# A diagonal state-space layer in blocks of four steps, with a turned scan over 128 blocks

## The chip, the cores and the metric

The kernel runs on one core of one Trainium2 chip. The metric is the device time of one execution in microseconds; the profile is one execution as the hardware profiler recorded it. PE is TensorE's matmul, PEld its weight load, DVE is VectorE, ACT ScalarE, POOL GpSimd, SP SyncE.

## The reference

A batch of one, 512 tokens, width 1024, in float32. Two layers of block 1 (neighbourhood attention, grouped attention, spatial gating, merged by gates) are followed by one layer of block 2. Block 2 projects the tokens to three branches of width 512: forgetting attention, a chunked state-space scan, and the diagonal state-space layer that is changed here. The gated sum of the branches is projected and normed; a convolutional feed-forward part ends the program. The diagonal layer has 32 groups of 16 channels with 64 complex states each:

```python
mag = jnp.exp(lam_re * step)
abar_re = mag * jnp.cos(lam_im * step)
abar_im = mag * jnp.sin(lam_im * step)
...
bu_re = jnp.einsum('blgh,gnh->lbgn', ug, bb_re)
bu_im = jnp.einsum('blgh,gnh->lbgn', ug, bb_im)
...
_, _, h_re, h_im = lax.associative_scan(
    _complex_linear_combine, (a_seq_re, a_seq_im, bu_re, bu_im), axis=0)
y = (jnp.einsum('lbgn,ghn->blgh', h_re, c_re.astype(f32))
     - jnp.einsum('lbgn,ghn->blgh', h_im, c_im.astype(f32)))
y = y.reshape(bsz, l, S5_WIDTH) + d_skip.astype(f32) * u.astype(f32)
gy = jax.nn.gelu(y)
out = gy * jax.nn.sigmoid(gy @ w_glu.astype(f32) + b_glu.astype(f32))
```

So each complex state follows h[t] = a h[t-1] + B u[t], over 512 steps, and y = Re(C h) + d u.

## The kernel before

Nearly all products are taken in two exact parts: `load_w` (L67) loads weights, ScalarE rounds the high part (L76), VectorE or GpSimd (by `lo_gp`) takes the low part (L78), and `mm3` (L99 to L101) issues three fp32r matmuls of 128 weights by 512 tokens per product. Sums go to PSUM banks by tag: three of "mm", two of "s", two of "t", one of "v". Tiles of 128 x 512 come from one pool ("b2", 36 buffers), tables and rows from another ("ld", 7). All DMAs are issued on SyncE.

Independent work is written as Python generators and interleaved by hand: `fill` (L165) advances a queue of projection jobs, and `step` advances the state-space branch. Within what the dependencies and the pools allow, a planner at compile time orders the instructions of each engine; every engine then takes its own queue in order.

`s5_params` (L1125) prepares the branch. It is a generator, advanced by the merges of block 1, one piece per 128 output columns. It computes magnitudes and phases, tables of cos and sin over 128 steps for the 16 tiles of 128 states (GpSimd, L1214 to L1222, to DRAM), the input matrices in two parts ("lbd") and the output matrices ("cc5").

`s5` (L1286) is advanced by block 2: 0.9 pieces per step of `fox`, 0.4 per step of `ssd`, 0.8 per step of the merges (RF, RS, RM). Each of 16 tiles of states takes: two input matmuls over 512 tokens (L1326), whose three stacked parts of the inputs are put together by small DMAs (L1315); a turn by the phase tables (L1331 to L1337, VectorE and GpSimd), which makes the recurrence real; eight scans of 128 steps with the magnitude as factor (L1355), with a carry between the four pieces of the sequence (L1347 to L1351); a turn back (L1362 to L1368); and output matmuls with 32 columns of fp32 weights (L1376). After every fourth tile comes the gelu. `prep` projects the inputs of four tiles and splits them.

`block2` (L1435) runs `fox`, `ssd`, the merges of branches 0 and 1, what is left of `s5`, then `glu` and the merge of branch 2. In a merge, L726 takes the gates and L741 empties a product's "mm" bank on VectorE. At the end of block 1 and later, `ln_tok` norms each token tile with a power on GpSimd (L247).

Of the kernel before, what the change touches and what calls it, by code (L numbers as in the profile page):

```python
# [19 lines left out]
P = 128  # L20
# [5 lines left out]
class Net:  # L26
    def __init__(self, ctx, tc, a, out, dump=None, upto=99):
# [11 lines left out]
        # weights' low parts: which of them GpSimd takes from VectorE, in turn  # L39
# [27 lines left out]
    def load_w(self, src):  # L67
        """weights in two exact parts"""
# [25 lines left out]
    def mm3(self, ps, ws, xs, first=True, last=True):  # L94
        """ps += sum over k of w^T x, with w and x in two exact parts each"""
# [7 lines left out]
    def fm(self, src, w=None):  # L103
        """features x tokens tile [128, 512] of x @ w for 128 columns of w"""
# [6 lines left out]
    def fm2(self, srcs):  # L111
        """two such tiles, by halves of the tokens"""
# [8 lines left out]
    def tm(self, srcs, use):  # L121
        """tokens x 256 columns tiles of x @ w; use(t, psum)"""
# [42 lines left out]
    def fill(self, n=1, drain=False):  # L165
        """advances the first of the queued generators"""
# [132 lines left out]
    def weights_T(self, e, n):  # L299
        """[128 queries, n keys] -> [128 keys, n / 128, 128 queries]"""  # L300
# [8 lines left out]
    def heads_q(self, src, scale=1.0):  # L309
        """fp32 [128,512] holding two heads -> per head 64 rows of high and 64 rows of low parts"""  # L310
# [9 lines left out]
    def heads_k(self, src):  # L320
        """the same for the keys: per head the high parts in both halves; the low parts of both heads"""
# [10 lines left out]
    def z_gate(self, bias_name, bi, out):  # L332
        """use of a projection tile: z * (1 + tanh(z / 2)) = 2 silu(z) goes into out, z = psum + b"""
# [10 lines left out]
    def gqa(self, l, zs):  # L344
        """zs: the gates, times which the outputs go into zs"""
# [3 lines left out]
        # values of two token tiles: [high 0, low 0, low 1, high 1] for the groups 0 and 1  # L349
# [36 lines left out]
        # rotation tables times the norms' gains: [128, 2 (cos|sin), 4, 64] for q and k  # L386
# [8 lines left out]
        def norm_rope(u, tc_, ts_, split):  # L395
            """[128, 8, 64] -> two tiles [128, 4, 2, 64] with each head twice"""
# [32 lines left out]
        def q_T(qo):  # L429
            qs = []  # L430
            for i in range(2):
# [3 lines left out]
                # rows 0-63 the high parts, rows 64-127 the low parts  # L435
# [15 lines left out]
        # heads in pairs of one group: their weights go through the values together  # L451
# [16 lines left out]
        def turn(i):  # L468
            """two key tiles of a pair's weights -> [128 keys, 2 tiles, (2 heads, 128 queries)], two parts"""
# [18 lines left out]
        def gate(t, i):  # L488
            """the sums' two parts, the bias and the gates of heads i, i + 1 and i + 4, i + 5"""
# [76 lines left out]
    def sgu(self, l, vn, uz, ys):  # L566
        """a generator"""
# [22 lines left out]
    def na(self, l, vd):  # L590
# [45 lines left out]
        def bias(i):  # L636
            """the relative positions' bias with the mask for step i"""
# [78 lines left out]
    def merge_gen(self, out, r, ys, wbr, gates, bname, b0, first=False, last=False, step=None):  # L716
        """acc += (1 + tanh(gate / 2)) * (y @ w) for one branch; the last gives the sum in two parts"""
# [150 lines left out]
    def bcast_row(self, ps, r, last=True):  # L868
        """ps[m, t] = row r of the cumulative sums, for every m"""
# [4 lines left out]
    def fox(self, xb, zz, step):  # L874
# [41 lines left out]
        js += [zj(i) for i in range(4)]  # L916
        self.queue.append(self.jobs(js))
# [7 lines left out]
        def weights(hp, t, s):  # L925
# [13 lines left out]
            # scores less the keys' sums; the query's sum is added to the maximum and to the exponent's bias  # L939
# [46 lines left out]
    def conv(self, ps, col, k, bias):  # L986
        """causal depthwise convolution over the tokens of a features x tokens tile"""
# [7 lines left out]
    def ssd(self, xb, zz, step):  # L995
# [3 lines left out]
        # ends of the chunks, on every partition  # L999
# [500 lines left out]
NB2 = 36  # L1500
# [177 lines left out]
```

## Time and profile before

| | before |
|---|---|
| median of 3 runs | 2070.54 us |
| lowest to highest | 2069.55 to 2071.32 us |
| span of the profiled execution | 2068.7 us |
| median of the runs less that span | 1.8 us |
| PE, DVE, ACT, POOL busy | 1996.5, 1407.4, 859.7, 515.1 us |
| mean granted TensorE clock | 0.989 |

The profile has no time of its own for the profiled execution beside its span, so its time is taken as the span and 1.8 us. Busy time of an engine is the union of its records; a matmul's records overlap, so 0.389 us long ones can follow each other every 0.225 us. Stretches are in us from the span's start. Block 2 begins at about 1120, and the merge of branch 2 ends at about 1650.

### The profile page before, as it was taken

How to read it: one execution, taken by the hardware profiler on the slowest of the kernel's cores; microseconds unless marked ns; L12 is line 12 of the kernel's file. 1: busy time of each engine (PE TensorE's matmuls, PEld its weight loads, DVE VectorE, ACT ScalarE, POOL GpSimd, SP SyncE). 2: the span in 40 equal slices, each digit the busy share in tenths (PEclk: the TensorE clock that was granted, in tenths of full speed). 3: DMA queues.
4: the chain of work that ended last, by engine and by line, in shares of the span. 5: the costliest groups of instructions: out<-in, count | busy, mean ns of one | idle time of the engine just before them, and what ended most of it. 6: DMA issues, size and time to landing. Idle time of an engine off the chain costs nothing. (4 is left out here: it accounts for less than half of the span.)

```text
span 2068.7 us, 29389 instructions
## 1 busy us (share of the span) xinstructions
PE 1996.5 (97%) x10402; PEld 1641.8 (79%) x10402; DVE 1407.4 (68%) x2857; ACT 859.7 (42%) x1742; POOL 515.1 (25%) x542
## 2 busy tenths in 40 slices
PE   7999999999999999999999999998979999999998
PEld 7898877788899888777888776766657888888888
DVE  7776646764667674567447688879997476645655
ACT  3455446433334553654233555532223334423431
POOL 3343211101324436123001334537660000000000
PEclk9999999999999999999999999999989999999999
DMA  6432233334343322333444222212313423333332
GB/s 211 150 98 72 74 97 106 106 94 126 117 153 90 99 74 82 110 112 124 137 126 148 83 70 69 73 34 93 91 62 111 132 85 106 96 97 97 101 86 69
DMA packets 127699, 209.88 MB, mean 101 GB/s; under 512 B 15936, under 2 KB 33344, under 8 KB 127552
## 3 DMA queue, kind: packets, MB, share of 16 engines
q1 hardware_dynamic: 127552, 208.01, 32.3%
q8 instruction: 82, 1.34, 0.3%
q14 instruction: 65, 0.53, 0.1%
HBM read 190.65 MB, written 14.16 MB: 99 GB/s over the span
## 5 line engine op out<-in xcount | busy, mean ns | idle before, releaser
L99 PE MATMUL psmm<-xh,wh 128*128 128x512 f32 (+1 forms) x1504 | 605.0, 403 | 32.2 <-DVE tmp L741 19.3
L76 ACT CAST wh<-wr 128x512 fp32r<-128x512 f32 x605 | 362.1, 618 | 605.5 <-PE psmm L100 296.1
L78 DVE TENSOR_TENSOR wl<-wr,wh 128x512 fp32r<-128x512 f32 x525 | 369.5, 714 | 334.4 <-ACT wh L76 330.5
L100 PE MATMUL psmm<-xl,wh 128*128 128x512 f32 (+1 forms) x1504 | 590.0, 392 | 0.3 <-DVE xl L262 0.3
L101 PE MATMUL psmm<-xh,wl 128*128 128x512 f32 (+1 forms) x1504 | 589.4, 392 | 0.0
L99 PEld LDWEIGHTS psmm<-xh,wh 128*128 128x128 f32 x1504 | 285.2, 190 | 97.8 <-DVE tmp L741 20.6
L101 PEld LDWEIGHTS psmm<-xh,wl 128*128 128x128 f32 x1504 | 284.7, 189 | 61.5 <-DVE wl L78 1.4
L100 PEld LDWEIGHTS psmm<-xl,wh 128*128 128x128 f32 x1504 | 285.7, 190 | 53.8 <-DVE xl L262 0.7
L247 POOL TENSOR_TENSOR sm<-sm,mhalf 128x1 f32<-128x1 f32 x20 | 18.9, 946 | 711.6 <-DVE sm L245 711.6
L100 PE MATMUL psmm<-wl,xh 128*128 128x256 f32 (+1 forms) x512 | 147.2, 288 | 2.8 <-DVE wl L78 2.5
L99 PE MATMUL psmm<-wh,xh 128*128 128x256 f32 (+1 forms) x512 | 148.1, 290 | 0.9 <-ACT xh L261 0.8
L101 PE MATMUL psmm<-wh,xl 128*128 128x256 f32 (+1 forms) x512 | 147.4, 288 | 0.3 <-DVE xl L262 0.2
L78 POOL TENSOR_TENSOR wl<-wr,wh 128x512 fp32r<-128x512 f32 x80 | 113.7, 1433 | 113.6 <-ACT wh L76 104.8
L465 POOL TENSOR_SCALAR b<-b,sm 128x512 f32<-128x512 f32 x64 | 100.4, 1570 | 163.9 <-DVE sm L296 147.7
L99 PE MATMUL psmm<-b,wh 128*128 128x512 f32 x304 | 120.2, 395 | 0.1
L100 PE MATMUL psmm<-b,wh 128*128 128x512 f32 x304 | 118.7, 390 | 0.0
L101 PE MATMUL psmm<-b,wl 128*128 128x512 f32 x304 | 118.5, 390 | 0.0
L100 PEld LDWEIGHTS psmm<-wl,xh 128*128 128x128 f32 x512 | 99.5, 194 | 4.8 <-DVE wl L78 3.6
L99 PEld LDWEIGHTS psmm<-wh,xh 128*128 128x128 f32 x512 | 99.4, 195 | 2.7 <-ACT xh L261 1.5
L101 PEld LDWEIGHTS psmm<-wh,xl 128*128 128x128 f32 x512 | 99.4, 194 | 0.8 <-DVE xl L262 0.8
L294 ACT ACTIVATE b<-pss,sm 128x512 f32<-128x512 f32 x64 | 44.1, 688 | 82.3 <-DVE sm L291 81.8
L647 POOL TENSOR_TENSOR b<-ld,namask 128x256 f32<-128x256 f32 x48 | 39.6, 850 | 154.2 <-PE pss L659 30.7
(375 smaller groups left out, 3495.3 us busy)
## 6 DMA issues: line engine op xcount, KB each, us to landing
wr<-in_w1fm SPq DMA_DIRECT2D x192, 256.0 KB
wr<-in_w2fm SPq DMA_DIRECT2D x92, 256.0 KB
wr<-in_wup SPq DMA_DIRECT2D x88, 256.0 KB
wr<-in_wbr SPq DMA_DIRECT2D x72, 256.0 KB
wr<-in_w1tm SPq DMA_DIRECT2D x56, 256.0 KB
wr<-in_wout SPq DMA_DIRECT2D x48, 256.0 KB
wr<-in_wdown SPq DMA_DIRECT2D x43, 256.0 KB
ld<-in_rows SPq DMA_DIRECT2D x32, 256.0 KB
```

What stands on the lines that cost most here:

```text
L76: nc.scalar.copy(hi[:, c], raw)
L78: eng.tensor_tensor(lo[:, c], raw, hi[:, c].bitcast(F32), op=ALU.subtract)
L99: mm(ps, wh, xh, start=(first and k == 0), stop=False)
L100: mm(ps, wh, xl, start=False, stop=False)
L101: mm(ps, wl, xh, start=False, stop=(last and k == n - 1))
L247: nc.gpsimd.tensor_tensor(rs, ve, self.mhalf[:, :1], op=ALU.pow)
L294: nc.scalar.activation(e[:, :n], src, AF.Exp, bias=nm, scale=scale, accum_out=sm)
L465: nc.gpsimd.tensor_scalar(e, e, r, None, op0=ALU.mult)
L647: nc.gpsimd.tensor_tensor(bms[i][:, s], bts[hp][s][:, :, x0:x0 + 32], self.namask[:, (0, 1, 1, 2)[j], None].to_broadcast([P, 8, 32]), op=A ...
```

## The change

The sequence is cut in 128 blocks of BT = 4 steps. A tile of inputs is regrouped so that its 128 partitions are 4 steps by 32 channels and its columns are the blocks. Input matrices ("lbd") hold B, aB, a^2 B, a^3 B, so one matmul of 128 rows gives what a block adds to a state; the scan runs over 128 blocks with the magnitude to the fourth and phase tables of the fourth power; output matrices ("cbd") give the four steps' outputs from the state at the block's start, and a triangular matrix ("dbd", the skip weight on its diagonal) gives the part inside the block. Four tiles of states go through one instruction of 512 columns, with a factor of zero at each tile's first block in place of carries. These matmuls are plain fp32, no longer in parts. The input projections become jobs of the queue in `fox`, and inputs and outputs are regrouped by writing them to DRAM ("usd", "ysd") and reading them back in another order. Preparation gains the matrices' powers, on VectorE and GpSimd, and small matmuls. The pool "b2" has 43 buffers, the pieces per step are 0, 0.5 and 1.5, and the compiler's scratch for DMAs of GpSimd is set to 1024 bytes.

```diff
@@ fox: the jobs of the queue
         js += [zj(i) for i in range(4)]
+        def uj(F):
+            return self.fm_job(fm[18 + F], lambda ps: self.s5_in(F, ps))
+        self.ub = {}
+        js += [uj(F) for F in range(4)]
...
+    def s5_in(self, F, pu):
+        nc = self.nc
+        u = self.b2()
+        nc.scalar.copy(u.rearrange("p (j b) -> p b j", j=BT), pu.rearrange("p (b j) -> p b j", j=BT))
+        nc.sync.dma_start(self.usd[F], u)
+        ub = self.b2(shape=(P, 4, P))
+        src = self.usd[F].rearrange("(i r) (j b) -> j r i b", r=32, j=BT)
+        for j in range(BT):
+            nc.sync.dma_start(ub[32 * j:32 * j + 32], src[j])
+        self.ub[F] = ub
@@ s5_params, after the tables
+        def cmul(eng, o, x, y, neg=False):
+            u1, u2 = (self.tmp(shape=(P, 16, 16)) for _ in range(2))
+            eng.tensor_tensor(u1, x[0], y[0], op=ALU.mult)
...
+        for j in range(BT - 1, -1, -1):
+            for h in range(2):
+                blk = self.b2(shape=(P, 2, 2, 2, 64))
+                for k in range(2):
...
+                    g.tensor_tensor(blk[:, :, k], src[:, :, None].to_broadcast([P, 2, 2, 64]), par.to_broadcast([P, 2, 2, 64]), op=ALU.mult)
+                for f in range(2):
+                    nc.sync.dma_start(self.lbd[2 * h + f, :, 32 * j:32 * j + 32], blk[:, f].rearrange("p k g n -> p (k g n)"))
+            if j:
+                nxt = self.b2(shape=(P, 2, 16, 16))
+                cmul(v, (nxt[:, 0], nxt[:, 1]), wide[2:], (cur[:, 0], cur[:, 1]))
+                cur = nxt
+            yield
...
+        cmul(g, (bd[:, 0], bd[:, 1]), tall[:2], (bn[:, 0], bn[:, 1]))
...
+        for k in range(BT):
+            nxt = self.b2(shape=(P, 2, 16, 16))
+            cmul(g, (nxt[:, 0], nxt[:, 1]), tall[2:], (ck[-1][:, 0], ck[-1][:, 1]), neg=True)
+            ck.append(nxt)
             yield
...
         for F in range(4):
...
+                spread(e0[:, 0, k], bd[:, k], F)
+                spread(e0[:, 1, k], ck[0][:, k], F)
+                for j in range(BT):
+                    spread(ce[k][:, :, j], ck[j + 1][:, k], F)
             yield
+            pl = self.psum("mm", (P, P))
+            for i in range(4):
+                for k in range(2):
+                    nc.tensor.matmul(pl[32 * i:32 * i + 32, 0:32], e0[:, 0, k, i].rearrange("p g c -> p (g c)"),
+                                     e0[:, 1, k, i].rearrange("p g c -> p (g c)"), start=(k == 0), stop=(k == 1))
...
@@ s5
+        for F in range(4):
+            while F not in self.ub:
+                self.fill(1)
+            ub = self.ub.pop(F)
+            mt = self.b2(shape=B4)
+            gp.tensor_copy(mt, self.magb[:, 4 * F:4 * F + 4, None].to_broadcast(list(B4)))
+            gp.memset(mt[:, :, 0:1], 0.0)
+            px = [self.psum(tags[0]) for _ in range(2)]
             for k in range(2):
+                for i in range(4):
+                    nc.tensor.matmul(px[k][:, i * P:i * P + P], w[i // 2][:, i % 2, k * P:k * P + P], ub[:, i], start=True, stop=True)
...
+            for x in (t0, t2):
+                y = x.rearrange("p i b -> p (i b)")
+                v.tensor_tensor_scan(y, mt.rearrange("p i b -> p (i b)"), y, initial=0.0, op0=ALU.mult, op1=ALU.add)
             yield
+            zr, zi, t1, t3 = (self.b2(shape=B4) for _ in range(4))
+            v.tensor_tensor(zr, t0, tb[0], op=ALU.mult)
+            v.tensor_tensor(t1, t2, tb[1], op=ALU.mult)
+            gp.tensor_tensor(zr, zr, t1, op=ALU.subtract)
...
+            for i in range(4):
+                q = slice(i * P, i * P + P)
+                nc.tensor.matmul(py[:, q], db[:, i], ub[:, i], start=True, stop=False)
+                for k, z in enumerate((zr, zi)):
+                    nc.tensor.matmul(py[:, i * P + 1:i * P + P], ce[k][:, i], z[:, i, 0:P - 1], start=False, stop=(k == 1))
...
+            dst = self.ysd[F].rearrange("(i r) (j b) -> j r i b", r=32, j=BT)
+            for j in range(BT):
+                nc.sync.dma_start(dst[j], y[32 * j:32 * j + 32].rearrange("p (i b) -> p i b", i=4))
+            backs[F] = self.b2()
+            nc.sync.dma_start(backs[F], self.ysd[F])
+            yield
+            if F:
+                close(F - 1)
                 yield
+        close(3)
@@ constants
-NB2 = 36
+NB2 = 43
-RF = 0.9
-RS = 0.4
-RM = 0.8
+RF = 0.0
+RS = 0.5
+RM = 1.5
+BT = 4
```

## Rows read from the trace of the kernel before

**Rows 1.** Page, part 1: busy us, share of the span, instructions.

```profile
PE 1996.5 (97%) x10402; PEld 1641.8 (79%) x10402; DVE 1407.4 (68%) x2857; ACT 859.7 (42%) x1742; POOL 515.1 (25%) x542
```

**Rows 2.** Busy time by stretches: length, then PE, PEld, DVE, ACT, POOL (records), clock, DMA.

```profile
850.00:950.00 100.00, 100.00 (x526) 75.04 (x525) 61.55 (x170) 56.76 (x128) 32.01 (x63) 1.00 0.34 101
...
1120.00:1200.00 80.00, 76.63 (x438) 64.26 (x437) 55.22 (x116) 40.27 (x86) 24.50 (x19) 0.98 0.39 125
1200.00:1395.00 195.00, 183.82 (x981) 135.37 (x979) 161.60 (x440) 95.60 (x243) 79.51 (x61) 0.98 0.19 58
1395.00:1600.00 205.00, 174.50 (x724) 133.37 (x725) 189.72 (x334) 54.15 (x95) 107.73 (x74) 0.93 0.29 89
1600.00:1650.00 50.00, 50.00 (x222) 41.40 (x221) 24.51 (x38) 18.02 (x32) 0.00 (x0) 1.00 0.40 128
```

**Rows 3.** Chain of waits, 1500 to 1540: start us, us, what.

```profile
1510.48 0.59 DVE tmp L741
...
1511.91 0.43 PE psmm L100
...
1514.64 0.23 PE psmm L101
```

**Rows 4.** Waits of PE, 1120 to 1600: us in total, times, longest.

```profile
PE psmm L99 <- DVE tmp L741: 19.3, 3, 10.1
PE psmm L99 <- ACT b L1300: 6.8, 2, 6.5
...
PE pst L304 <- ACT b L947: 3.7, 4, 1.9
PE pst L862 <- DVE b L859: 3.2, 1, 3.2
```

**Rows 5.** Groups by line, 1120 to 1600, VectorE.

```profile
L1355 DVE TENSOR_TENSOR_SCAN b<-mag,inx,b 128x128 f32<-128x128 f32 x96 | 53.0, 583 | 0.0
L1355 DVE TENSOR_TENSOR_SCAN b<-mag,b 128x128 f32<-128x128 f32 x32 | 29.6, 940 | 2.6 <-POOL b L1336 1.5 <-POOL b L1337 1.1
...
L1367 DVE TENSOR_TENSOR b<-b,ld 128x512 f32<-128x512 f32 x16 | 21.7, 1354 | 0.0
...
L1351 DVE SCALAR_TENSOR_TENSOR inx<-b,s,inx 128x1 f32<-128x1 f32 x48 | 16.7, 347 | 0.0
...
L1362 DVE TENSOR_TENSOR b<-b,ld 128x512 f32<-128x512 f32 x16 | 15.0, 936 | 0.0
...
L1331 DVE TENSOR_TENSOR b<-psmm,ld 128x512 f32<-128x512 f32 x9 | 6.2, 683 | 0.9 <-PE psmm L1326 0.9
```

**Rows 6.** Groups by line, 1120 to 1600, PE; last, L1376 alone by stretch.

```profile
L974 PE MATMUL psv<-acc,b 128*128 128x64 f32 x160 | 22.3, 270 | 0.0
...
L1077 PE MATMUL pst<-b,b 128*64 128x128 f32 x64 | 6.1, 282 | 0.1
...
1120.00:1600.00 480.00, 17.66 (x64) 3.47 (x64) 0.96 0.26 82
```

**Rows 7.** Single lines, VectorE: min/median/max ns, first and last start us.

```profile
L859 DVE TENSOR_TENSOR_SCAN b<-ld,b x1: 1225/1225/1225, 1152.6 to 1152.6; 128x512 f32<-128x512 f32 x1
...
L1362 DVE TENSOR_TENSOR b<-b,ld x16: 657/688/1708, 1209.1 to 1554.9; 128x512 f32<-128x512 f32 x16
```

**Rows 8.** GpSimd: groups by line from 760 and from 1120; busy time 960 to 1080.

```profile
L647 POOL TENSOR_TENSOR b<-ld,namask 128x256 f32<-128x256 f32 x24 | 19.1, 820 | 65.0 <-PE pss L659 30.7 <-DVE sm L664 15.2 <-ACT tmp L606 14.9
...
L498 POOL TENSOR_TENSOR b<-b,b 128x128 f32<-128x128 f32 x8 | 3.5, 463 | 3.5 <-DVE b L495 3.5
...
L78 POOL TENSOR_TENSOR wl<-wr,wh 128x512 fp32r<-128x512 f32 x80 | 113.7, 1433 | 113.6 <-ACT wh L76 104.8 <-DMA wr<-in_w2fm 8.5 <-PE psmm L1326 0.2
...
960.00:1080.00 120.00, 0.49 (x1) 1.00 0.44 138
```

**Rows 9.** Chain of waits: a copy of inputs, issue on SyncE and landing.

```profile
1447.96 0.57 SPq L1315
1448.60 2.62 DMA b<-b
```

More of the change, by code (lines that the diff above doesn't have):

```diff
@@ L1205, in s5_params @@
             cw, sw = n1, n3
-            yield
+            if k % 2:
+                yield
+        t1, t2, den = new(), new(), new()
+        v.tensor_tensor(t1, lre, lre, op=ALU.mult)
+        v.tensor_tensor(t2, ai, ai, op=ALU.mult)
+        v.tensor_tensor(den, t1, t2, op=ALU.add)
+        v.reciprocal(den, den)
+        are, aim = new(), new()
+        v.tensor_tensor(are, mag, cs, op=ALU.mult)
+        v.tensor_tensor(aim, mag, sn, op=ALU.mult)
+        am1 = new()
+        v.tensor_scalar(am1, are, -1.0, None, op0=ALU.add)
+        yield
+        kre, kim = new(), new()
+        v.tensor_tensor(t1, am1, lre, op=ALU.mult)
+        v.tensor_tensor(t2, aim, ai, op=ALU.mult)
+        v.tensor_tensor(t1, t1, t2, op=ALU.add)
+        v.tensor_tensor(kre, t1, den, op=ALU.mult)
+        v.tensor_tensor(t1, aim, lre, op=ALU.mult)
+        v.tensor_tensor(t2, am1, ai, op=ALU.mult)
+        v.tensor_tensor(t1, t1, t2, op=ALU.subtract)
+        v.tensor_tensor(kim, t1, den, op=ALU.mult)
+        yield
+        g = nc.gpsimd
         self.tabd = self.dr.tile([4, 2, P, 512], F32, name="tabd")
-        g = nc.gpsimd
         for F in range(4):
@@ new lines, in s5_params @@
+        br = self.ld(shape=(P, 2, 16, 16))
+        for i in range(2):
+            nc.sync.dma_start(br[:, i].rearrange("p a b -> p (a b)"), a["s5b"][i])
+        wide = [x[:, :256].rearrange("p (a b) -> p a b", a=16) for x in (kre, kim, are, aim)]
+        cur = self.b2(shape=(P, 2, 16, 16))
+        cmul(v, (cur[:, 0], cur[:, 1]), wide[:2], (br[:, 0], br[:, 1]))
+        yield
+        self.lbd = self.dr.tile([4, 4, P, 256], F32, name="lbd")
+        par = self.col("par", 0, 2)[:, None, :, None]
@@ new lines, in s5_params @@
+        bn = self.ld(shape=(P, 2, 16, 16))
+        c0 = self.ld(shape=(P, 2, 16, 16))
+        for i in range(2):
+            nc.sync.dma_start(bn[:, i], a["s5bn"][i])
+            nc.sync.dma_start(c0[:, i], a["s5c"][i])
+        tall = [x[:, 256:, None].to_broadcast([P, 16, 16]) for x in (kre, kim, are, aim)]
+        bd = self.b2(shape=(P, 2, 16, 16))
+        cmul(g, (bd[:, 0], bd[:, 1]), tall[:2], (bn[:, 0], bn[:, 1]))
+        ck = [c0]
+        v.tensor_scalar(c0[:, 1], c0[:, 1], -1.0, None, op0=ALU.mult)
@@ new lines, in s5_params @@
+            for i in range(4):
+                for k in range(2):
+                    nc.tensor.matmul(pl[32 * i:32 * i + 32, 32:P], e0[:, 0, k, i].rearrange("p g c -> p (g c)"),
+                                     ce[k][:, i, 0:BT - 1].rearrange("p j g c -> p (j g c)"), start=(k == 0), stop=(k == 1))
+            lg = self.b2(shape=(P, P))
+            v.tensor_copy(lg, pl)
+            v.scalar_tensor_tensor(lg[:, 0:32], self.col("eye32", 0, 32), self.col("sd", F), lg[:, 0:32], op0=ALU.mult, op1=ALU.add)
@@ L1321, in inputs, with load @@
-        def inputs(u):
-            F, i = divmod(u, 4)
-            lb, ub = us.pop(u)
-            pb = [self.psum(tags[0]) for _ in range(2)]
+        backs = {}
+        def load(F):
+            w = [self.b2(shape=(P, 2, 256)) for _ in range(2)]
+            for h in range(2):
+                nc.sync.dma_start(w[h], self.lbd[F, 2 * h:2 * h + 2].rearrange("i p n -> p i n"))
+            tb = [self.ld(B4) for _ in range(2)]
+            for i in range(2):
+                nc.sync.dma_start(tb[i].rearrange("p i t -> p (i t)"), self.tabd[F, i])
+            return w, tb
@@ new lines, in load2, with close @@
+        def load2(F):
+            ce = [self.ld(B4) for _ in range(2)]
+            for i in range(2):
+                nc.sync.dma_start(ce[i].rearrange("p i t -> p (i t)"), self.cbd[F, i])
+            db = self.ld(B4)
+            nc.sync.dma_start(db, self.dbd[F].rearrange("i p n -> p i n"))
+            return ce, db
+        def close(F):
+            yn = backs.pop(F)
+            nat = yn.rearrange("p (j b) -> p b j", j=BT)
+            hi, lo = self.b2(F32R), self.b2(F32R)
+            h3, l3 = (x.rearrange("p (b j) -> p b j", j=BT) for x in (hi, lo))
+            nc.scalar.mul(h3, nat, 0.5)
+            v.scalar_tensor_tensor(l3, nat, 0.5, h3.bitcast(F32), op0=ALU.mult, op1=ALU.subtract)
+            gys.append((hi, lo))
@@ L1325, in inputs @@
+        w, tb = load(0)
+        yield
+        for F in range(4):
[6 more added lines that the diff above has]
+            px = [self.psum(tags[0]) for _ in range(2)]
             for k in range(2):
-                nc.tensor.matmul(pb[k], lb[:96, k * P:k * P + P], ub[:96], start=True, stop=True)
@@ L1327, in inputs @@
[L1327 to L1328 removed]
+                for i in range(4):
+                    nc.tensor.matmul(px[k][:, i * P:i * P + P], w[i // 2][:, i % 2, k * P:k * P + P], ub[:, i], start=True, stop=True)
+            pr, pi = (x.rearrange("p (i b) -> p i b", i=4) for x in px)
             t0, t1, t2, t3 = (self.b2(shape=B4) for _ in range(4))
[L1330 to L1331 removed]
@@ L1391, in s5 @@
-        prep(0, None)
-        yield
-        yield
-        load(0)
-        for _ in range(3):
-            yield
-        w = None
-        for u in range(18):
-            if u < 16:
-                if u % 4 == 1 and u < 12:
-                    w = self.load_w(fm[19 + u // 4])
-                if u % 4 == 2 and u < 12:
-                    prep(u // 4 + 1, w)
-                yield from inputs(u)
-                if u < 15:
-                    load(u + 1)
-            if 0 < u < 17:
-                for b in range(4):
-                    scans(u - 1, b)
-                    yield
-                yield from states(u - 1)
-            if u > 1 and u % 2 == 1:
-                outputs(u - 2)
+            v.tensor_tensor(zi, t0, tb[1], op=ALU.mult)
@@ new lines, in s5 @@
+            v.tensor_tensor(t3, t2, tb[0], op=ALU.mult)
+            gp.tensor_tensor(zi, zi, t3, op=ALU.add)
+            if F < 3:
+                w, tb = load(F + 1)
+            yield
+            py = self.psum(tags[1])
+            for i in range(4):
+                q = slice(i * P, i * P + P)
+                nc.tensor.matmul(py[:, q], db[:, i], ub[:, i], start=True, stop=False)
+                for k, z in enumerate((zr, zi)):
+                    nc.tensor.matmul(py[:, i * P + 1:i * P + P], ce[k][:, i], z[:, i, 0:P - 1], start=False, stop=(k == 1))
```

189 lines of the change are left out of this document (53 added, 136 removed).

## The prediction

> **What bounds the kernel now.** I read the page first: TensorE is busy for 97% of the span [rows 1], so whatever shortens the kernel has to come out of TensorE's time. An average over a program of many stages says little, so the second view is the busy time by stretches [rows 2]. In the attention of block 1 (850:950) TensorE is busy for all of its 100 us, and at 1600:1650 too, at 222 matmul records in 50 us, 0.225 us each. The stretch in which block 2 works on its three branches is different. It runs from 1120 to 1600, 480 us, and I cut it in three: projections and the start of the forgetting attention, the rest of attention with the chunked scan, the merges of the first two branches. TensorE is idle there for 3.4, 11.2 and 30.5 us, 45 in all, and its granted clock falls to 0.98, 0.98 and 0.93. VectorE, meanwhile, is busy 55 of 80, 162 of 195 and 190 of 205 us. In the last of the three it has no room left.
>
> The chain of waits says the same from the end of the kernel back: before 1600 it runs along VectorE, and hands over to TensorE where a product is taken out of PSUM [rows 3]. At 1510.48 VectorE reaches L741, which empties a bank of "psmm" that TensorE needs; the matmuls that follow go at 0.43 us each, and by 1514.64 at 0.23. That is the lower and then the full level of TensorE's clock (1.2 and 2.4 GHz): a wait of TensorE is paid twice, once idle and once slow. The list of TensorE's waits puts sizes to it [rows 4]: 19.3 us in three waits behind VectorE's L741 and 6.8 behind a ScalarE read of the bank of a state-space projection, all in the merges; 3.7 and 3.2 us are attention's and the step logits' own.
>
> What fills VectorE is the diagonal state-space branch [rows 5]: 128 scans of 128 columns (53.0 + 29.6 us), five lines of one-column carries between them (48 each, the dearest 16.7 us), four lines that turn the states back (16 each, 15.0 to 21.7 us), and 64 turns of the inputs at 0.68 us. Roughly 83 + 65 + 70 + 44, an estimate of 260 us of VectorE's 407 in the stretch.
>
> **The change part by part.** *VectorE.* Sixteen tiles of states over 512 steps become four groups of four tiles over 128 blocks. A group has four turns of inputs from PSUM (4 x 0.68), two scans of 512 columns, four turns of the states, and some four instructions for the output. A 512-column scan is shown once, at 1.225 us [rows 7]. The turns back take 0.69 us in the median and 1.71 at most [rows 7]; four are 2.8 to 6.8. With 2.8 for the rest a group is 2.7 + 2.5 + 2.8 to 6.8 + 2.8, 11 to 15 us; four are 43 to 59. So about 200 us leave VectorE, and the carries' chain of short dependent instructions goes entirely. By itself this is worth what TensorE waited for.
>
> *The merges, 1395:1600.* 724 records at 0.225 are 163 us [rows 2]; 42 of the 205 us are wait and low clock. I leave 5 for what remains and take -37. The bounds are -42 and, if only the waits behind L741 vanish, -19.
>
> *Attention and the chunked scan, 1120:1395.* Idle time is 14.6 us, and 2% of clock in 275 us is 5 more. The state-space pieces leave attention (RF is 0), and the four projections of the state-space inputs, until now at its own pace, become fill for the chunked scan, which had none. The waits that are attention's own stay (3.7 and 3.2 us) [rows 4]. I take -18; bounds -5 and -25 (some short gaps count as busy).
>
> *TensorE's own work.* Removed are 32 input matmuls in one pass, at 0.225 us 7.2 us, and the output matmuls, 17.7 us [rows 6]. Their replacements are plain fp32. The trace shows such a matmul as two records: 64 for the 32 of L1376, 160 for the 80 of L974. Added are 8 + 12 matmuls a group, 160 records with 128 x 128 weights. The nearest row is L974, the same weights with 64 columns: 22.3 / 160 = 0.14 us; I take that, 22 us; the bounds are L1077's 0.095 (6.1 / 64, narrower weights) and 0.27, the mean duration of one: 15 and 43. Sixty-four more matmuls with 32-column weights move into the preparation, in block 1, where nothing hides them: 128 records at 0.08, just under L1077, 10 us; bounds 6 and 18. Sum: +7, from -4 to +36.
>
> *Preparation on GpSimd.* It gains 16 spreads of the input matrices and 30 instructions of complex products, of 256 columns each, and 48 spreads of 128 columns: by L647's 0.82 and L498's 0.46 us [rows 8] 46 x 0.82 + 48 x 0.46 = 60 us. The cover is that GpSimd is nearly idle (0.5 us busy) from 960 to 1080, when the last pieces of preparation run. The pieces come by the merges of block 1, one per 128 output columns and in close pairs, so each group's spreads (12 x 0.46 = 5.5 us) can be only one piece ahead of the matmuls that read them, and TensorE takes its queue in order. I take 3 us, bounds 0 and 12 (three in each group). VectorE's part there is hidden: TensorE is 100% busy and VectorE about half.
>
> *DMAs.* The 48 copies of 64 KB that stack the parts of the inputs go. For each group come one write of the inputs to DRAM and four strided reads, four strided writes of the outputs and one read, and on SyncE all of these stand ahead of weights. One hop shows as 0.57 us on SyncE and 2.62 to land [rows 9]; a round trip is two hops, 6.4 us, and more if the strides are slow. The inputs' trip lies between the projection and the use, several pieces apart; the outputs' trip is closed one group later, and the last has all of branch 1's merge behind it. I cost them at 0. Without that cover it is 6 us for each of eight trips; one or two may show. The seven more buffers only allow more work ahead: 0.
>
> *SBUF between engines.* GpSimd keeps splitting weights in the merges (1.43 us each, 80 of them) [rows 8], while VectorE turns states; L1362 then takes 1.71 instead of 0.69 us [rows 7]. The Trainium skill, "SBUF — State Buffer", section "Who interferes with whom", has the rule: a VectorE instruction with two SBUF inputs and a GpSimd instruction that reads SBUF exclude each other for a whole instruction, and the loser fully blocks. The trace agrees with it here. By that rule the turns after the change would cost the upper price above throughout, since their pace (1.5 pieces per merge step) puts them beside the splits: VectorE's sum for the branch would be 59 us by the rule and 43 by the row's median, and TensorE's sum moves only if the first rival below holds.
>
> **The sum.** -37 - 18 + 7 + 3 = -45. The profiled span of 2068.7 becomes 2023.7; the median of the runs is 1.8 above that span, which I add unchanged: 2025.
>
> **The rivals.** *Half of it.* TensorE still waits in the merges, now for the group's chain: matmul, turn, GpSimd sum, scan, turn, GpSimd sum, matmul. Three groups run within a third of the first merge, some 16 of its steps of six matmuls, 16 x 6 x 0.225 = 22 us, more with the group's own matmuls. VectorE then has 33 to 45 us to do in about 30, GpSimd the weights' splits and four 1.5 us sums a group. If the excess of 15 us is paid and attention gives only its lower 5, the sum is -37 + 15 - 5 + 7 + 3 = -17: 2053. The upper price of the turns beside GpSimd's splits is what pushes here. For it: VectorE and GpSimd both busy [rows 2]. Against it: what follows, branch 1's merge, has no such work, and the excess can be taken from there.
>
> *Slower.* The place is the end of block 1. Its layer norm takes a power on GpSimd, in the queue behind the preparation. If the 60 us of spreads and products aren't done when the last merge ends at about 1080, TensorE waits for the normed tokens. It decides when the backlog passes the gain of some 45 us; with all 60 in a lump, 2025 + 60 = 2085. For it: preparation's GpSimd work already ran in lumps between 760 and 960. Against: 120 us of nearly idle GpSimd before that norm.
>
> *No change.* The chain's last stage would have been TensorE anyway: if the idle time were only displaced into the attention's own waits, and the fp32 matmuls cost their upper 36 us, -37 - 5 + 36 + 3 gives 2067. Against: the 850:950 stretch shows such an attention, with fills and no scans, at 100 of 100 us.
>
> **How the numbers follow.** Forecast 0.62 (2000 to 2042), half of it 0.24 (2042 to 2062), no change 0.05, slower 0.09. The likeliest gives 2025. The low end 2000 is the lower bounds, -42 - 25 - 4 + 0 = -71, which give 2000; the high end 2056 takes in most of the half case and leaves out some 2 in 10. Within 0.2% (about 4 us, what a measurement of this kernel can tell from none) lies part of the no-change case: 0.04. Faster 0.87, slower 0.09.
>
> **What would show it.** Right: VectorE's busy time between 1120 and the start of branch 2's merge falls from 407 to 200 to 220 us; the waits behind L741 are gone; the granted clock there is 1.00 and the stretch is some 50 us shorter; TensorE in block 1 is busy throughout, with about 10 us of new small matmuls. Wrong: a wait of TensorE for a GpSimd spread near 1000 or for the layer norm near 1100; a wait for a DMA at the input matmuls; fp32 records above 0.2 us each; turns of states at 1.7 us with TensorE idle beside them.

## The result and the profile after

| | before | after |
|---|---|---|
| median | 2070.93 us | 2042.95 us |
| lowest to highest | 2069.55 to 2073.49 us | 2042.89 to 2046.97 us |
| span of the profiled execution | 2068.7 us | 2041.1 us |

The ratio is 0.9869, interval 0.9855 to 0.9883: 28 us faster where 45 were forecast. That is in the range, but just past the forecast's own end of 2042, in the region of the rival "half of it".

First the ledger, from one line that both programs have: L741 takes each of a merge's eight products out of PSUM, so its last record in a merge marks the end of that merge. The sums are differences of its start times.

| stretch | before, us | after, us | difference | forecast |
|---|---|---|---|---|
| start to the last merge of block 1 | 1073.4 | 1081.9 | +8.5 | +13 |
| from there to the first L741 of block 2 | 332.5 | 314.8 | -17.6 | together -58 |
| the three merges of block 2 | 244.1 | 225.6 | -18.5 | |
| the rest | 418.7 | 418.7 | 0 | 0 |

(The forecast's +13 is 10 for small matmuls and 3 for spreads; -58 is -37 - 18 and what then remains of TensorE's own +7.) So block 1 came out 4.5 us better than forecast and block 2's branches 22 us worse. The page and the stretches, as in [rows 1, 2]:

```profile
PE 1988.1 (97%) x10594; PEld 1653.3 (81%) x10594; DVE 1236.0 (61%) x2406; ACT 863.2 (42%) x1738; POOL 509.8 (25%) x594
```

```profile
1129.00:1573.00 444.00, 421.44 (x2203) 341.98 (x2202) 221.26 (x422) 194.37 (x421) 143.39 (x112) 0.97 0.32 100
...
1397.00:1500.00 103.00, 86.07 (x393) 71.67 (x392) 48.01 (x54) 29.57 (x49) 53.54 (x40) 0.90 0.40 125
1500.00:1575.00 75.00, 75.00 (x332) 62.12 (x331) 33.28 (x50) 26.06 (x45) 13.94 (x11) 1.00 0.32 100
```

VectorE did nearly what was forecast (200 to 220): 221 us in the first of these, which runs up to branch 2's merge, where it had 407 [rows 2]. Yet TensorE still idles 17 us of the 103 at the start of the merges, with a clock of 0.90, and none from 1500 on. TensorE's waits there (us in total, times, longest) against [rows 4]:

```profile
PE pst L1440 <- POOL b L1427: 15.7, 3, 6.2
PE pst L862 <- DVE b L859: 3.6, 1, 3.6
PE pst L304 <- ACT b L952: 0.9, 1, 0.9
PE pst L1440 <- POOL b L1431: 0.8, 1, 0.8
```

The 19.3 us behind L741 and 6.8 behind ScalarE are gone. New are 16.5 us at L1440, the output matmuls of the branch, which wait for a group's sums (L1427, L1431), once in each of groups 1 to 3 and, for L1431, a second time in group 3; group 0, which runs beside the chunked scan, has none. The groups by line from 1120 to 1600:

```profile
L1440 PE MATMUL pst<-b,ld 128*128 128x127 f32 x48 | 12.0, 383 | 16.4 <-POOL b L1427 15.7 <-POOL b L1431 0.8
...
L1438 PE MATMUL pst<-b,ld 128*128 128x128 f32 x24 | 6.6, 369 | 0.5 <-DMA ld<-dbd 0.4
L1408 PE MATMUL pss<-b,b 128*128 128x128 f32 x48 | 6.4, 277 | 0.0
...
L1422 DVE TENSOR_TENSOR_SCAN b<-b,b 128x512 f32<-128x512 f32 x8 | 15.3, 1917 | 6.0 <-POOL b L1416 6.0
L1427 POOL TENSOR_TENSOR b<-b,b 128x512 f32<-128x512 f32 x4 | 6.2, 1557 | 6.0 <-DVE b L1426 6.0
```

How one such wait comes about is seen in the timeline of group 1 (start, us, engine, line; in brackets the idle time before and what ended it):

```profile
1391.23 0.68 DVE L1411 TENSOR_TENSOR b<-pss,ld 128x512 f32<-128x512 f32 x1
...
1393.19 1.30 POOL L1416 TENSOR_TENSOR b<-b,b 128x512 f32<-128x512 f32 x1 [3.57 <-DVE b L1414]
1394.45 1.30 POOL L1417 TENSOR_TENSOR b<-b,b 128x512 f32<-128x512 f32 x1
1394.53 2.30 DVE L1422 TENSOR_TENSOR_SCAN b<-b,b 128x512 f32<-128x512 f32 x1 [0.82 <-POOL b L1416]
1395.71 4.35 POOL L78 TENSOR_TENSOR wl<-wr,wh 128x512 fp32r<-128x512 f32 x2
1397.33 1.67 DVE L1422 TENSOR_TENSOR_SCAN b<-b,b 128x512 f32<-128x512 f32 x1
1398.92 1.68 DVE L1425 TENSOR_TENSOR b<-b,ld 128x512 f32<-128x512 f32 x1
1400.53 0.68 DVE L1426 TENSOR_TENSOR b<-b,ld 128x512 f32<-128x512 f32 x1
...
1401.29 1.64 POOL L1427 TENSOR_TENSOR b<-b,b 128x512 f32<-128x512 f32 x1 [1.23 <-DVE b L1426]
...
1402.98 0.79 PE L1440 MATMUL pst<-b,ld 128*128 128x127 f32 x2 [4.70 <-POOL b L1427]
1403.43 0.77 PE L100 MATMUL psmm<-xl,wh 128*128 128x512 f32 x1
1404.00 0.63 PE L101 MATMUL psmm<-xh,wl 128*128 128x512 f32 x1
1404.43 0.63 PE L99 MATMUL psmm<-xh,wh 128*128 128x512 f32 x1
```

The chain from the first turn (L1411) to the first output matmul takes 11.75 us, 11.7 in group 2 and 13.3 in group 3. Three things in it are long. The GpSimd sums take 1.30 and 1.64. The scans take 2.30 and 1.67 where [rows 7] had 1.225. The first turn back takes 1.68. TensorE meanwhile holds matmuls of the merge (L100, with weights that L99 has just used) *behind* L1440 in its queue, and the first of them come 0.43 us apart, the lower of the clock's two levels (1.2 and 2.4 GHz), where they came 0.225 apart before the wait.

The slow instructions fit the rule that the prediction drew on (the Trainium skill, "SBUF — State Buffer", section "Who interferes with whom": a VectorE instruction with two SBUF inputs and a GpSimd instruction that reads SBUF exclude each other). The first scan starts 0.08 us after GpSimd's L1417 and lasts 1.09 us longer than the 1.21 that it takes without company below, with 1.22 of L1417 left; the two splits L78, beside the second scan and the turn, take 4.35 instead of 2.54 (the pair at 1413.14). The trace agrees.

Block 1 has the small matmuls of the preparation (940 to 1100):

```profile
L1334 PE MATMUL psmm<-b,b 128*32 128x96 f32 x64 | 2.4, 249 | 0.0
L1330 PE MATMUL psmm<-b 128*32 128x32 f32 x64 | 2.1, 202 | 0.0
```

They are 4.5 us, where 10 were costed. The other part of the +8.5 stood in no step of the prediction. It begins at the end of layer 0, in ScalarE's timeline:

```profile
519.96 0.69 ACT L726 ACTIVATE tmp<-psmm,hcols 128x512 f32<-128x512 f32 x1 [6.86 <-POOL b L1250]
```

L726, a gate, waits 6.9 us for a buffer of the three "tmp" that GpSimd's phase tables hold (L1245 to L1250, now in one long piece); the casts of weights (L76) stand behind it on ScalarE, and TensorE then waits 2.2 us for one of them, once between 515 and 600, where the kernel before has no such wait.

### The profile page after: what moved, and what is told of

Its sections match the earlier page's. It is cut to its first block, busy times and chain, and to the rows that moved or that the text cites. A ratio compares the mean times of both kernels' runs of the same rounds, so it can differ in the third digit from the quotient of the medians.

```text
span 2041.1 us, 29326 instructions
## 1 busy us (share of the span) xinstructions
PE 1988.1 (97%) x10594; PEld 1653.3 (81%) x10594; DVE 1236.0 (61%) x2406; ACT 863.2 (42%) x1738; POOL 509.8 (25%) x594
## 5 line engine op out<-in xcount | busy, mean ns | idle before, releaser
L76 ACT CAST wh<-wr 128x512 fp32r<-128x512 f32 x605 | 362.1, 618 | 587.5 <-PE psmm L100 273.7
L99 PE MATMUL psmm<-xh,wh 128*128 128x512 f32 (+1 forms) x1504 | 604.3, 402 | 1.5 <-DVE b L373 1.4
L100 PE MATMUL psmm<-xl,wh 128*128 128x512 f32 (+1 forms) x1504 | 588.1, 391 | 0.3 <-DVE xl L262 0.3
L78 DVE TENSOR_TENSOR wl<-wr,wh 128x512 fp32r<-128x512 f32 x526 | 374.6, 723 | 348.9 <-ACT wh L76 341.4
L99 PEld LDWEIGHTS psmm<-xh,wh 128*128 128x128 f32 x1504 | 284.1, 189 | 60.8 <-issue 3.4
L100 PEld LDWEIGHTS psmm<-xl,wh 128*128 128x128 f32 x1504 | 284.4, 189 | 52.7 <-DVE xl L262 0.7
L78 POOL TENSOR_TENSOR wl<-wr,wh 128x512 fp32r<-128x512 f32 x79 | 109.7, 1401 | 229.2 <-ACT wh L76 228.7
L99 PE MATMUL psmm<-wh,xh 128*128 128x256 f32 (+1 forms) x512 | 148.3, 291 | 2.0 <-DVE b L373 1.3
L100 PE MATMUL psmm<-wl,xh 128*128 128x256 f32 (+1 forms) x512 | 147.1, 287 | 2.0 <-DVE wl L78 1.8
L99 PE MATMUL psmm<-b,wh 128*128 128x512 f32 x304 | 119.8, 394 | 0.0
L100 PE MATMUL psmm<-b,wh 128*128 128x512 f32 x304 | 118.6, 390 | 0.0
L99 PEld LDWEIGHTS psmm<-wh,xh 128*128 128x128 f32 x512 | 99.4, 195 | 4.0 <-DVE b L373 1.7
L100 PEld LDWEIGHTS psmm<-wl,xh 128*128 128x128 f32 x512 | 99.5, 194 | 3.8 <-DVE wl L78 2.6
```

Source lines behind the costliest of these rows:

```text
L76: nc.scalar.copy(hi[:, c], raw)
L78: eng.tensor_tensor(lo[:, c], raw, hi[:, c].bitcast(F32), op=ALU.subtract)
L99: mm(ps, wh, xh, start=(first and k == 0), stop=False)
L100: mm(ps, wh, xl, start=False, stop=False)
```

## The experiments

Ratios are to the kernel before on the same chip: 2070.6 us, or 2069.3 for four of the runs (the tied load, `close` last, `NLD = 10` alone, GpSimd out alone). The theories behind the letters are told in the expectations.

**Is it the buffers?** The kernel before, with 43 buffers and the scratch of 1024 bytes alone.

```diff
-NB2 = 36
+NB2 = 43
...
-    nc = bacc.Bacc("TRN2", target_bir_lowering=False, num_devices=1)
+    nc = bacc.Bacc("TRN2", target_bir_lowering=False, num_devices=1, dynamic_dma_scratch_size=1024)
```

> The kernel before with two things of the change alone: 43 buffers instead of 36, and the compiler's scratch for GpSimd's DMAs at 1024 bytes. My forecast costs them at nothing: within 3 us of 2070. If buffers held work back in the merges (the turns of a next tile): 2055 to 2066.

Measured: 2068.67 us, ratio 0.9991 (0.9982 to 1.0000). The buffers by themselves are worth nothing that can be told.

**Is VectorE's relief the gain (theory F)?** A first kernel put a 512-column scan of an own buffer, which nobody reads, at each step of block 2; a second tied its scans to results, 64 to attention's weights and 80 to the merges' sums. Both have 42 buffers. The edit shown is the second one's.

```diff
+    def more(self, n, src):
+        if self.dd is not None:
+            for _ in range(n):
+                self.nc.vector.tensor_tensor_scan(self.dd, src[:, 0:1].to_broadcast([P, 512]), self.dd, initial=0.0, op0=ALU.mult, op1=ALU.add)
...
+                    if r < 2:
+                        self.more(5, acc)
...
+            self.more(2, e)
```

> The changed kernel with VectorE's load of before put back: one more 512-column scan of a buffer of its own (about 1.2 us, read by nothing) at each of the 180 steps of attention, chunked scan and merges that advance the diagonal layer, some 220 us in all, and 42 buffers instead of 43. Theory F (the 36 us that block 2 gained were VectorE's load): the time goes back to 2065 to 2085, with TensorE waiting behind VectorE's L741. Rival G (the gain came from the carries' chain, the inputs' small DMAs and the regrouped projections, not from the load): 2043 to 2052.

> The changed kernel with about 175 us of VectorE's load put back where it was: 512-column scans that nothing reads, each fed by a column of attention's weights (two for each of the 32 steps) or of a merge's sum (five for each of 16), so that they can't run earlier, and 42 buffers. Theory F (what block 2 gained is VectorE's load): the time goes back to 2065 to 2090, TensorE waits behind L741 again. Rival G (the gain came with the carries, the inputs' small DMAs and the regrouped projections): 2043 to 2055.

The first gave 2196.99 us and tells nothing of block 2: with no input from there, the scans ran in block 1, whose last merge ended at 1235.7 instead of 1081.9. The second gave 2101.94 us, 1.0159 (1.0142 to 1.0176), 59 us above the kernel after and above its expectation; its scans took 203.8 us, not 175. Its stretches and its largest waits of TensorE:

```profile
1130.00:1430.00 300.00, 269.40 (x1483) 209.69 (x1485) 228.81 (x389) 137.21 (x328) 90.66 (x65) 0.98 0.26 82
1430.00:1610.00 180.00, 153.27 (x659) 124.25 (x660) 174.59 (x153) 48.40 (x82) 82.44 (x48) 0.90 0.31 98
```

```profile
PE pst L1449 <- POOL b L1436: 19.2, 3, 7.6
PE pst L992 <- ACT yt L989: 11.5, 9, 1.7
PE pst L310 <- ACT b L960: 10.1, 11, 1.8
PE psmm L106 <- DVE b L94: 6.9, 1, 6.9
...
PE psmm L105 <- DVE tmp L747: 3.6, 1, 3.6
```

(Lines are moved by the edit: L1449 is L1440, L747 is L741, L310 is L304.) With VectorE as full as before (403 us in these 480, before 407), the 36 us that block 2's branches had gained are gone (595.6 us from block 1's last merge to the last L741, before 576.6, after 540.4), and the new wait at the output matmuls stays on top. So that much load on VectorE does cost TensorE its time, and rival G as stated, in which the load costs nothing, falls. But the scans do not bring back the waits of before: L741 has 3.6 us where it had 19.3, and 21.6 us are waits of attention behind ScalarE, where the kernel after had 0.9, since two scans now stand behind each step's weights and five behind each sum. That the carries and the small DMAs had no part in the 36 us is therefore not shown.

**What is the wait at L1440?** Four edits, each against one part of it. (1) The output matmuls four pieces later in the program:

```diff
-            yield
+            for _ in range(5):
+                yield
             py = self.psum(tags[1])
```

> The changed kernel with the output matmuls of each group of the diagonal layer given out four pieces later, so that the last complex sum on GpSimd is long done when TensorE comes to them. Theory A (in the merges TensorE stands in its queue behind a group's own chain, 16.5 us of waits at the output matmuls plus the low clock after them): those waits fall under 3 us, the granted clock in 1400 to 1500 goes from about 0.9 to 0.98 or more, and the time falls by 15 to 25 us, to 2018 to 2028. Theory B (the merges are held by the weights' splits on GpSimd or by the fp32 matmuls themselves, and the waits at the output matmuls only stand in for that): another wait of the same size appears and the time stays within 5 us of 2043.

2039.19 us, 0.9852 (0.9836 to 0.9869). The wait for L1427 is 16.7 us, before the edit 15.7. The edit did not move what it was meant to move: the output matmuls of groups 1 to 3 come 11.7 to 13.6 us after the group's first turn (before the edit 11.7 to 13.3), and only those of group 0, which never waited, come later (1380.1 instead of 1361.3). So the run decides nothing about theory A or B. It shows that later in the program need not be later in the queue; that the planner goes by when an instruction can run is the likely reason, and isn't shown.

(2) The two sums behind the turn back on VectorE:

```diff
-            gp.tensor_tensor(zr, zr, t1, op=ALU.subtract)
+            v.tensor_tensor(zr, zr, t1, op=ALU.subtract)
...
-            gp.tensor_tensor(zi, zi, t3, op=ALU.add)
+            v.tensor_tensor(zi, zi, t3, op=ALU.add)
```

> The changed kernel with the two complex sums after the turn back (zr and zi) moved from GpSimd to VectorE, which is idle about half of the merges. It shortens the chain ahead of the output matmuls by two GpSimd instructions of 1.3 to 1.6 us and by what stands ahead of them in GpSimd's queue. Theory A (the chain sets TensorE's wait): each of the three waits loses 1.5 to 3 us, the time falls by 4 to 10 us, to 2033 to 2039. Theory C (the wait is VectorE's scans and turns, which run slowly beside GpSimd's splits): the two sums on VectorE at 0.7 to 1.7 us each give nothing, within 3 us of 2043.

2039.06 us, 0.9849 (0.9834 to 0.9864). The wait falls to 13.2 (three times, now for VectorE's L1427), the chain from 11.75 to 11.2. That is 3.2 us less wait, under theory A's 4.5 to 9, and from block 1's last merge to the end of the merges the time is 539.5 us against 540.4. The remaining 3 us lie in block 1, which the edit doesn't touch, so the run supports neither theory by itself.

(3) Theory H: the next group's turns come late, since `close` of the group before, which takes its outputs back from DRAM and splits them (L1393 on ScalarE, L1394 on VectorE), stands ahead of them. So `close` only after the last group:

```diff
-            if F:
-                close(F - 1)
-                yield
-        close(3)
+        for _ in range(12):
+            yield
+        for F in range(4):
+            close(F)
+            yield
```

> The changed kernel with the four groups' outputs taken back from DRAM and split (L1393 on ScalarE, L1394 on VectorE) only after the last group, instead of each one group later. Theory H (the output matmuls wait because the next group's turns L1411 stand in VectorE's queue behind L1394, which stands behind late weights on ScalarE; 9.6 us between a group's input matmuls and its first turn): L1411 starts within 2 us of its input matmuls, the waits at L1440 fall from 15.7 to under 5 us, the time by 10 to 18 us, to 2025 to 2033. Theory A2 (the chain of scans and turns itself is longer than the planner allowed for): the waits stay above 10 us and the time within 4 us of 2043.

2038.97 us, 0.9856 (0.9843 to 0.9869). The turns of group 2 come at 1410.65 instead of 1420.76, as meant, but the waits are still 14.1 + 0.8 us. GpSimd's timeline shows why:

```profile
1416.13 1.29 POOL L78 TENSOR_TENSOR wl<-wr,wh 128x512 fp32r<-128x512 f32 x1 [2.40 <-ACT wh L76]
...
1417.42 1.29 POOL L78 TENSOR_TENSOR wl<-wr,wh 128x512 fp32r<-128x512 f32 x1
1418.67 1.29 POOL L1416 TENSOR_TENSOR b<-b,b 128x512 f32<-128x512 f32 x1
```

The turns end at 1413.1, and the sum L1416 stands behind splits of weights that wait for ScalarE: the chain of group 2 is 16.8 us here. Theory H falls: the time and the waits are those that its rival A2 names.

(4) Theory I: weights come late, because SyncE's queue stands at loads that wait for a buffer of "ld". So `NLD = 10` for 7.

> The changed kernel with 10 buffers for rows and tables instead of 7. Theory I (SyncE's queue, which also brings the weights, stands still at L1385 until the previous group's output matmuls give back a buffer: 9.4 us in two waits, behind which weights are late, and behind these ScalarE): those waits go, the waits at L1440 fall by a third or more, the time falls by 5 to 12 us. Rival (the waits for VectorE's output at L1451, 7.4 us, hold the same weights anyway): within 3 us of 2043.

2038.16 us, 0.9848 (0.9834 to 0.9861). SyncE's 9.4 us at L1385 are gone, but 8.7 us of waits for the same output matmuls now stand at other loads (L176, L1383), so the edit moved this wait more than it removed it. L1440's wait is 16.2, and from block 1's last merge to the end of the merges it is 538.4 us against 540.4. Nothing speaks for theory I, and the expected 5 to 12 us did not come there; but this is not a clean test of it.

**GpSimd (theory J).** Out of the merges altogether: no splits of weights there, and all four sums of a group on VectorE. Then the splits alone.

```diff
-            gp.tensor_tensor(t0, t0, t1, op=ALU.add)
-            gp.tensor_tensor(t2, t2, t3, op=ALU.subtract)
+            v.tensor_tensor(t0, t0, t1, op=ALU.add)
+            v.tensor_tensor(t2, t2, t3, op=ALU.subtract)
... (and the two sums of the edit above)
-        self.lo_gp = (1,)
+        self.lo_gp = (0,)
```

> The changed kernel with GpSimd taken out of the merges of branches 0 and 1: the weights' low parts and the four complex sums of each group go to VectorE. Theory J (GpSimd's splits stretch the scans to 2.3 us and the turns to 1.7, and hold the buffers of raw weights): scans at 1.2 and turns at 0.7 us, the waits at L1440 under 8 us, 2028 to 2036. If theory H alone holds (the order in the queues, not GpSimd): scans and turns are as short, but the waits stay at 10 us or more and the time within 5 us of 2039.

> The changed kernel with only the weights' low parts of the merges of branches 0 and 1 on VectorE; the four complex sums stay on GpSimd. Theory J1 (the splits in GpSimd's queue, each behind a ScalarE rounding and a weight load, hold the group's sums, and stretch scans and turns): nearly all of the 17 us that came with GpSimd out of the merges, 2026 to 2031, waits at L1440 under 5 us. Theory J2 (the sums themselves, 1.3 to 1.6 us each and two in a row twice in the chain, are as much of it): 2031 to 2037, waits at L1440 of 5 us or more.

All of it: 2026.26 us, 0.9795 (0.9782 to 0.9809), more than theory J expected. The splits alone (the last edit): 2032.53 us, 0.9815 (0.9802 to 0.9829), with 11.4 us of waits, as J2 has it: splits and sums both count. The same group without GpSimd, and its stretch:

```profile
1394.81 0.68 DVE L1411 TENSOR_TENSOR b<-pss,ld 128x512 f32<-128x512 f32 x1
...
1397.21 0.68 DVE L1416 TENSOR_TENSOR b<-b,b 128x512 f32<-128x512 f32 x1
1397.81 0.68 DVE L1417 TENSOR_TENSOR b<-b,b 128x512 f32<-128x512 f32 x1
1398.41 2.33 DVE L1422 TENSOR_TENSOR_SCAN b<-b,b 128x512 f32<-128x512 f32 x2
1400.66 0.66 DVE L1425 TENSOR_TENSOR b<-b,ld 128x512 f32<-128x512 f32 x1
...
1402.45 0.68 DVE L1427 TENSOR_TENSOR b<-b,b 128x512 f32<-128x512 f32 x1
```

```profile
1397.00:1500.00 103.00, 98.82 (x481) 82.12 (x480) 69.41 (x105) 35.33 (x59) 0.72 (x2) 1.00 0.46 146
```

VectorE does more (69 us for 48), yet the chain is 8.4 us, the wait at L1440 is 0.5 (2.8 us at L1438, for the load of "dbd", come up in its place), and TensorE issues 481 matmul records in these 103 us instead of 393 with its clock at 1.00. From block 1's last merge to the end of the merges it is 524.8 us, 15.6 less than in the kernel after. With the splits alone moved, the timeline shows the intermediate case: the first scan still takes 2.30 beside GpSimd's second sum, the second one and the first turn back 1.21 and 0.66:

```profile
1392.85 1.29 POOL L1417 TENSOR_TENSOR b<-b,b 128x512 f32<-128x512 f32 x1
...
1392.92 2.30 DVE L1422 TENSOR_TENSOR_SCAN b<-b,b 128x512 f32<-128x512 f32 x1 [0.87 <-POOL b L1416]
...
1395.72 1.21 DVE L1422 TENSOR_TENSOR_SCAN b<-b,b 128x512 f32<-128x512 f32 x1
1396.86 0.66 DVE L1425 TENSOR_TENSOR b<-b,ld 128x512 f32<-128x512 f32 x1
```

The chains of these kernels, groups 1 to 3 added up, against their waits for L1427: 36.8 us of chain and 15.7 of wait after, 33.6 and 13.2 with two sums moved, 30.8 and 11.4 with the splits moved, 25.4 and 0.5 without GpSimd. The difference, what TensorE has to do beside a group, is 7.0, 6.8 and 6.5 us a group on average in the first three and 8.3 in the last. So in these four the matmuls' place in the queue hardly moves, and a shorter chain is a shorter wait. With `close` last it is otherwise: 44.0 us of chain and 14.1 of wait, since there the first turns of groups 2 and 3 come 8 to 10 us earlier and the output matmuls only 5 to 6. What counts is when the chain ends, not its length alone.

**The tables' buffers.** t1 and t2 of the phase tables from the "b2" pool:

```diff
-                t1, t2 = (self.tmp(shape=(P, 4, 64))[:, :, :w] for _ in range(2))
+                t1, t2 = (self.b2(shape=(P, 4, 64))[:, :, :w] for _ in range(2))
```

> The changed kernel with the two temporaries of the phase tables (preparation, GpSimd) taken from the pool of 43 buffers instead of the three short-lived ones that the merges' gates also use. Theory D (in block 1, near 513 to 520, a gate on ScalarE waits 6.9 us for a table's temporary and the weights' high parts wait behind it, so that TensorE loses about 5 us): the last merge of layer 0 ends at 523 instead of 529, and the time falls by 4 to 6 us, to 2037 to 2039. Rival E (the 5 us are made up by other slack before the end of block 1, or come from the new small matmuls): within 2 us of 2043.

2040.99 us, 0.9854 (0.9839 to 0.9868), with a profiled span 5.8 us shorter. The last merge of layer 0 ends at 523.65 instead of 528.85, layer 1's at 1077.2 instead of 1081.9, and the stretch from 535 to 560 first after, then here, is

```profile
535.00:560.00 25.00, 22.65 (x98) 18.13 (x96) 13.81 (x22) 4.29 (x8) 12.36 (x26) 0.93 0.32 109
```

```profile
535.00:560.00 25.00, 24.99 (x115) 20.42 (x114) 16.85 (x30) 4.51 (x8) 4.56 (x4) 1.00 0.24 84
```

17 records are 3.8 us: most of the 4.7. The cause is shown by the trace and by the edit; the median alone, 2 us lower with intervals that overlap, would not show it, and lies between theory D's 4 to 6 us and rival E (the profiled execution is the lowest of the four).

**The best version.** GpSimd out of the merges and the tables' buffers; then `NLD = 10` as well.

> GpSimd out of the merges, as in the run before with 2026, and the phase tables' temporaries from the pool of 43 buffers. If the two gains are in different places and nothing later is waiting, they add: the last merge of layer 0 ends near 523 and the time is 2020 to 2023. If the second is made up elsewhere: 2025 to 2028.

> As the run with GpSimd out of the merges and the tables' temporaries moved, and 10 buffers for rows and tables. With 7, SyncE waited 30 us for a turn to give back such a buffer while GpSimd was out of the merges; if weights behind it reach TensorE late, this gains 2 to 4 us more, 2017 to 2020; if TensorE has no waits left in the merges there, it gains nothing: within 2 us of the run without it.

2024.43 us, 0.9775 (0.9762 to 0.9788), and 2022.69 us, 0.9769 (0.9756 to 0.9783). That is 48 us below the kernel before and 20 below the kernel after. The first lies between its two expectations; in the trace the gains are in different places, as expected (layer 0 ends at 523.5, and 525.6 us pass from block 1's last merge to the end of the merges). What NLD adds is within what the runs can tell.

## Why the prediction was half right

**What bounds the kernel** held as far as the runs go: the waits behind L741 went with VectorE's load, and as much load put back, though in another place, costs more than the whole gain (2101.94). **Buffers** nothing, **DMA trips** nothing (0.4 us at L1438), **no backlog** before the layer norm: as costed.

**The merges** are the step that failed: of 205 us, 42 were "wait and low clock. I leave 5 for what remains". The waits behind L741 went, but 16.5 us of new ones came, in the place and by the chain that "half of it" names. The step compared sums of busy time (11 to 15 us of VectorE for a group; group 1's instructions add up to about 13), and these fit easily. What counts is the latency of one group: turn, GpSimd sum, scan, turn, GpSimd sum follow one another, 11.75 us, while some 7 us of TensorE's work stand ahead of the matmuls that wait for it, and all that could fill the gap stands behind them. The rival had the mechanism, but its price, 15 us, came from a sum of VectorE's work too; and the argument against it, that the next merge can take up the excess, was wrong because TensorE takes its queue in order: L100 stood ready behind L1440. With attention's -18 in place of the -5 that the rival gave it, its own sum is 2040, close to the 2043 measured.

Of the prediction's signs of being right, the clock in the stretch came out at 0.97 and not 1.00, and it is 36 us shorter, not 50. Of its signs of being wrong, two came, both in the merges: turns of states at 1.7 us with TensorE idle beside them, and fp32 records above 0.2 us (12.0 / 48 at L1440).

**Attention and chunked scan**: -18 forecast, -17.6 measured, but the match is in part luck. The -18 was for waits and low clock alone. In that stretch TensorE's idle time fell by 9.6 us (15.3 to 5.6), and the branch's own records in it went from 14.1 to 7.8 us, since more of its output matmuls now fall in the merges (14.7 to 18.3 us there). That leaves some -11 for waits and clock. The prediction's own rows give no more: 14.6 + 5 less the 3.7 and 3.2 that "stay" is 12.7. By the same count the merges gave some -22 where -37 was forecast.

**TensorE's own work** was priced well: 22 us for the 160 fp32 records, 26.1 measured (the union of L1408, L1438 and L1440), and 22.0 without GpSimd, where no wait lowers the clock. The price of one depends on the clock: here are four of group 0, which has no wait, and four of group 1 after its wait. The 48 of groups 1 to 3, which took 12.0 us in all (above), take 8.0 without GpSimd:

```profile
1367.40 0.61 PE L1440 MATMUL psmm<-b,ld 128*128 128x127 f32 x4
...
1407.41 1.06 PE L1440 MATMUL pst<-b,ld 128*128 128x127 f32 x4
```

```profile
L1440 PE MATMUL pst<-b,ld 128*128 128x127 f32 x48 | 8.0, 279 | 0.6 <-DVE b L1427 0.5
```

So the excess of 4 us is a part of the merges' miss and no second cause. The 128 small records took 4.5 us instead of 10. The output matmuls of before were priced by their union, 17.7, the input matmuls by their pace, 7.2; the union of both is 28.8, so by one measure the branch's records in block 2 fell by 2.7 us, where 22 - 24.9 = -3 was forecast. The 22 us by which block 2 missed are thus nearly all waits and low clock: some 15 in the merges, which come back when GpSimd is taken out (15.6 in block 2's branches), and some 7 in attention. Records overlap with their neighbours', so the parts are rough.

**Preparation**: no TensorE wait for spreads, where 3 us were put. Instead some 5 us at the end of layer 0 came from the tables' hold on "tmp" buffers, which the prediction didn't name: it counted GpSimd's time, not the buffers that its longer pieces keep.

Open: why edits that touch block 2 only shift block 1's end by 1 to 3 us (the planner's order changes there too; it wasn't isolated). With `NLD = 10`, which acts in the whole program, it is 5.5. Of the four edits at L1440 none changes the stretch from block 1's last merge to the end of the merges by more than 2.2 us, so the differences between the kernels at 2038 to 2043 are not explained one by one.

## What to carry to other kernels

When a bound engine is relieved, don't stop at its busy time: write out the chain of one group, with each instruction at its price beside its neighbours, and compare it with the work that stands ahead of the waiting instruction in the next engine's queue. An engine that helps out can lengthen that chain more than it relieves: here taking GpSimd out of the merges gave 15 to 17 us, though VectorE then did 45% more in the stretch. And a longer piece of side work is to be counted by the buffers it holds, not by its engine's time alone.

## What the runs showed of the hardware that was not expected

A VectorE scan of 128 x 512 takes 1.19 to 1.22 us alone and 2.30 when it starts just after a GpSimd sum; both engines pay, as the pair of splits shows (4.35 us against 2.54). Records of fp32 matmuls with 128 columns of weights follow each other every 0.21 us at the lower of the clock's two levels (four of them from 1407.41 to 1408.26) and every 0.11 at the higher (1367.40 to 1367.85). Those with 32 columns of weights came out at 0.035 us each (4.5 / 128), well under the 0.095 of [rows 6], but they also move fewer columns, 32 or 96 for 128.
